# The softmax division of layer 0 moved from VectorE to GpSimd in a two-layer encoder

## The chip, the cores and the metric

The kernel runs on one core of a Trainium2 chip, in one launch. The metric is device time in microseconds: the kernel before took 577.2 us (median of 3 runs, 576.47 to 578.21).

## What is computed

A batch of one sequence of 256 tokens, 1024 wide, goes through two residual layers. Layer 0 has two attention mixers with 8 heads each (A: grouped-query, B: dilated with a relative bias), whose outputs are concatenated and projected. Layer 1 has latent attention with 16 heads. Each layer ends with a squared-ReLU MLP of width 4096. The part that the change touches is the softmax of every head:

```python
logits = jnp.einsum('bqgrd,bkgd->bgrqk', qb, k).astype(jnp.float32) * scale
p = jax.nn.softmax(logits, axis=-1).astype(v.dtype)
return jnp.einsum('bgrqk,bkgd->bqgrd', p, v)
```

In mixer B the three dilated branches are merged into one softmax over all 256 keys, with a bias on the logits.

## The kernel before

Everything is float32 accuracy. Weights come in 1 MB chunks (`raw`, L210) and are split into a high and a low part, a piece of 128x1024 at a time: ScalarE makes `whi` (L222), VectorE subtracts it from `raw` to get `wlo` (L223, two inputs, both in SBUF). Projections are three matmuls each (`mm3`, L263 to L265: high by high, high by low and low by high).

`attention` (L343) treats 16 heads of 256 queries by 256 keys in one pipeline. For a head `h`:

- `scores(h)`: TensorE writes logits, 128 queries by 256 keys twice, into a PSUM bank (tile `s`, two banks; L853 and L854, four matmuls a head in layer 0).
- `maxima(h)`: VectorE takes row maxima. For the heads of mixer A (heads 0 to 7) this is one reduction of the bank (L422) and a product with the scale (L423). For those of mixer B (heads 8 to 15) it is two fused add-and-max instructions that write the biased logits into `prob` (L870, each with a small read of its accumulator), and a negation (L873).
- `exps(h)`: ScalarE writes the exponentials into `prob`, with row sums (L427 for A, L879 for B).
- `norm(h)`: VectorE takes the reciprocals of the row sums (L365, two columns of 128) and multiplies the two 128x256 halves of `prob` by it in place (L367, twice a head).
- TensorE transposes the four 128x128 blocks of `prob` (L395, tile `o`). The first block needs the first half of `prob`, the second the second half. ScalarE copies the result to `pts` (L398).
- `values(j)`: for each pair of heads, four matmuls with the values (L384), then a high and a low part of the output (`OT`, L386 on ScalarE and L387 on VectorE).

`prob` has three buffers, so `maxima` or `exps` of head h+3 write where head h was transposed. In the loop the order of issue is: transposes of h, `scores(h+2)`, `maxima(h+2)`, `norm(h+1)`, a part of the filler, `values` of the pair before, the rest of the filler, `exps(h+2)`. The filler is work for TensorE that does not depend on the heads in hand: the value projection of mixer B (`vB`, matmuls named `mm<-..,hTs`), then the first half of the output projection (matmuls named `mm<-..,OT`).

```python
        def norm(h):
            if h < n:
                r = small(2)
                nc.vector.reciprocal(r, sums[h])
                for i in range(NT):
                    nc.vector.tensor_scalar(prob[h][:, i], prob[h][:, i], r[:, i:i + 1], None, op0=OP.mult)
```

The code is written for a scheduler: it orders the instructions of each engine at build time by what it thinks they take and by priorities (`tc.high_priority`), and adds the semaphore waits. On the chip each engine then runs its own list strictly in that order. So another engine for one step also moves the other steps. GpSimd does small work only: in layer 0 the row scales until some 43 us, then nothing until the mean square at 120 us (L331).

Of the kernel before, what the change touches and what calls it, by code (L numbers as in the profile page):

```python
# [15 lines left out]
OP = mybir.AluOpType  # L16
# [12 lines left out]
HA = 8  # L29
HB = 8  # L30
HC = 16
# [135 lines left out]
def encoder(ctx: ExitStack, tc: tile.TileContext, x, xt, wall, gcol, grow, const, onehot, relb, out):  # L167
    nc = tc.nc
# [13 lines left out]
    def s_bank():  # L182
        return psum("s", 2)

    def t_bank():
        return psum("o", 2)

    def o_bank():
        return psum("o", 2)

    def small(n, bufs=4):
        return sp.tile([P, n], F32, name=f"sm{n}", tag=f"sm{n}", bufs=bufs)
# [48 lines left out]
    def take(name, j, n, whole=True):  # L241

        i = at["take"]
        assert ORDER[i] == (name, j), (ORDER[i], name, j)
        at["take"] += 1
        while whole and at["piece"] < 4 * i + 4:
            split_piece()

        def operand(k, c=slice(None)):
            half, kk = divmod(k, n // 2)  # L250
            return tuple(z.rearrange("p (k c) -> p k c", k=n // 2)[:, kk, c] for z in parts[i, half])

        return i, operand
# [3 lines left out]
    def cols(i, n=P):  # L257
        return slice(i * n, i * n + n)
# [81 lines left out]
            nc.tensor.matmul(bank[:, which * S + t * P:which * S + t * P + P], ones, dg, start=True, stop=True)  # L340


    def attention(heads, fill, dst):  # L343
        n = len(heads)
        sb, prob, sums, pts = {}, {}, {}, {}

        def scores(h):
            if h < n:
                sb[h] = s_bank()
                heads[h]["scores"](sb[h])  # L350

        def maxima(h):
            if h < n:
                prob[h] = sp.tile([P, NT, S], F32, name="prob", tag="prob", bufs=3)
                sums[h] = small(2)
                heads[h]["max"](h, sb[h], prob[h])

        def exps(h):
            if h < n:
                heads[h]["exp"](h, sb.pop(h), prob[h], sums[h])  # L360

        def norm(h):
            if h < n:
                r = small(2)
                nc.vector.reciprocal(r, sums[h])  # L365
                for i in range(NT):
                    nc.vector.tensor_scalar(prob[h][:, i], prob[h][:, i], r[:, i:i + 1], None, op0=OP.mult)  # L367

        scores(0)
        fill(-1, 0)  # L370
        maxima(0)
        exps(0)
        scores(1)
        fill(-1, 1)
        norm(0)
        maxima(1)
        exps(1)
        def values(j):

            ob = o_bank()  # L380
            with tc.high_priority(60):
                for c in range(NT):
                    for s in range(2):
                        nc.tensor.matmul(ob[64 * s:64 * s + 64, :S], heads[2 * j + s]["v"](c),  # L384
                                         pts[2 * j + s][:, cols(c, S)], start=c == 0, stop=c == NT - 1)
            nc.scalar.copy(dst[0][:, j], ob[:, :S])  # L386
            nc.vector.tensor_tensor(dst[1][:, j], ob[:, :S], dst[0][:, j].bitcast(F32), op=OP.subtract)  # L387

        for h in range(n):
            flipped = heads[h]["flip"]  # L390
            pt = t_bank()
            for c in range(NT):
                for i in range(NT):
                    q = NT - 1 - i if flipped else i
                    turned = nc.tensor.transpose(pt[:, c * S + q * P:c * S + q * P + P], prob[h][:, i, cols(c)],  # L395
                                                 flip if flipped else ident)
            pts[h] = sp.tile([P, 512], F32, name="pts", tag="pts", bufs=3)
            nc.scalar.copy(pts[h], pt)  # L398
            with tc.high_priority(20):
                scores(h + 2)  # L400
            with tc.high_priority(100):
                maxima(h + 2)
            norm(h + 1)
            with ExitStack() as order:
                if h >= n - 2:
                    order.enter_context(tc.issue_after(turned.ins))
                fill(h, 0)
            if h % 2 == 0 and h > 0:
                values(h // 2 - 1)
            fill(h, 1)  # L410
            with tc.high_priority(20):
                exps(h + 2)
        fill(n, 0)
        values(n // 2 - 1)

    def scaled_softmax(scale, nscale):

        nb = {}

        def mx(h, sb, p):  # L420
            m, nb[h] = small(2), small(2)
            nc.vector.reduce_max(m, halves(sb), axis=AX.X)  # L422
            nc.vector.tensor_tensor(nb[h], m, nscale, op=OP.mult)  # L423

        def ex(h, sb, p, l):
            for i in range(NT):
                nc.scalar.activation(p[:, i], sb[:, cols(i, S)], AF.Exp, bias=nb[h][:, i:i + 1],  # L427
                                     scale=scale[:, i:i + 1], accum_out=l[:, i:i + 1])

        return {"max": mx, "exp": ex, "flip": False}  # L430
# [204 lines left out]
    with tc.tile_pool(name="l0", bufs=1) as lp:  # L635
# [17 lines left out]
        OT = [ap.tile([P, KT, S], F32R, name=f"OT{i}", tag=f"OT{i}") for i in range(2)]  # L653
# [13 lines left out]
        with tc.manual_schedule():  # L667
# [3 lines left out]
            for j in range(2):  # L671
                i, w = take("qA", j, 4, whole=False)
                for k in range(4):
# [5 lines left out]
                                                   op0=OP.mult, op1=OP.subtract)  # L679
# [12 lines left out]
        i, w = take("kvA", 0, 8)  # L692
# [156 lines left out]
        def scores_two(q, kd, kl, s, j, order):  # L849
            def f(sb):  # L850
                for i in range(NT):
                    o = sb[:, cols(i, S)]
                    nc.tensor.matmul(o, q[s][:, j, cols(order[i])], kd, start=True, stop=False)  # L853
                    nc.tensor.matmul(o, q[s][:, j, cols(order[i])], kl, start=False, stop=True)  # L854
            return f

        def head_a(h):
            j, s = divmod(h, 2)
            return {"scores": scores_two(qA, kdA[:, s], klA[:, s], s, j, (0, 1)),
                    "v": lambda c: vA[:, c, cols(s, 64)],  # L860
                    **scaled_softmax(fq[:, 2 * j + s], nfq[:, 2 * j + s])}

        def head_b(h):
            j, s = divmod(h, 2)
            nb = {}

            def mx(n, sb, p):
                m, nb[0] = small(2), small(2)
                for i in range(NT):
                    nc.vector.tensor_tensor_reduce(  # L870
                        out=p[:, i], in0=sb[:, cols(i, S)], in1=bias[j][:, s, i * P:i * P + S],
                        op0=OP.add, op1=OP.max, scale=1.0, scalar=-3.0e38, accum_out=m[:, i:i + 1])
                nc.vector.tensor_scalar(nb[0], m, -1.0, None, op0=OP.mult)  # L873
                if s == 1 and j < 2:
                    load_bias(j + 2)

            def ex(n, sb, p, l):
                for i in range(NT):
                    nc.scalar.activation(p[:, i], p[:, i], AF.Exp, bias=nb[0][:, i:i + 1],  # L879
                                         accum_out=l[:, i:i + 1])  # L880

            return {"scores": scores_two(qB, kdB[:, h], klB[:, h], s, j, (1, 0)), "max": mx, "exp": ex,
                    "v": lambda c: vB[:, c, cols(h, 64)], "flip": True}
# [14 lines left out]
        def fill(h, part):  # L898
            if phase[0] == 0:
                n = 1 if h < 7 else 100  # L900
            else:
                n = SHARE_AB[h - 8] if part == 0 and h < 16 else 0
            if h < 0:
                n = 1
            for _ in range(n):
                r = next(fl, None)
                if r == "second":
                    phase[0] = 1
                    return
                if r is None and n == 100:  # L910
                    return
# [7 lines left out]
            pass  # L919
        for _ in mixer_a_keys(keys[0]):  # L920
            pass
        attention([head_a(h) for h in range(HA)] + [head_b(h) for h in range(HB)], fill, OT)
        for _ in fl:
            pass

# [4 lines left out]
    with tc.tile_pool(name="l1", bufs=1) as lp:  # L930
# [8 lines left out]
        OT = [ap.tile([P, KT, S], F32R, name=f"OT{i}", tag=f"OT{i}") for i in range(2)]  # L939
# [22 lines left out]
        for j in range(2):  # L962
            i, w = take("down", j, 4)
# [114 lines left out]
        def head_c(h):  # L1078
            def scores(sb):
                for i in range(NT):  # L1080
                    nc.tensor.matmul(sb[:, cols(i, S)], qT[:, h, cols(i)], kT[:, h], start=True, stop=True)  # L1081
            return {"scores": scores, "v": lambda c: vC[:, c, cols(h, 64)], **soft}

        soft = scaled_softmax(sc, nsc)
        attention([head_c(h) for h in range(HC)], fill, OT)
        for _ in fl:
            pass

# [36 lines left out]
```

## Time and profile before

| what | value |
|---|---|
| median of 3 runs | 577.2 us |
| the profiled execution | 577.27 us |
| its span | 575.2 us |
| TensorE matmuls busy | 559.3 us (97%) |
| VectorE busy | 397.0 us (69%) |
| ScalarE busy | 329.4 us (57%) |
| GpSimd busy | 37.3 us (6%) |
| the chain that ended last, by engine | PE 86%, DVE 5%, ACT 3% |

The span runs from the first to the last instruction; the 2.1 us between it and the execution's time lie around it. A busy time is the union of an engine's instructions. Matmuls overlap and their ends are modelled, so the distance between the starts of two matmuls tells more than their lengths. In the rows below DVE is VectorE, ACT ScalarE, PE TensorE, POOL GpSimd.

### The profile page before, as it was taken

To read this page: it belongs to the slowest core of one execution; us is meant where nothing else is said; L and a number is where in the kernel's file an instruction comes from. 1 tells how busy PE (TensorE), PEld (TensorE's weight loads), DVE (VectorE), ACT (ScalarE), POOL (GpSimd) and SP (SyncE) were. 2 spreads that over 40 slices of the span, in tenths; PEclk is the share of its full clock that TensorE was granted. 3 is DMA by queue.
4 is the path that set the end of the run, shared out by engine and by line. 5 is a ranking of instruction groups with operands and counts; after the bars stand their busy time and mean duration, and the time that the engine had idled before them with its cause. 6 is when DMAs were issued, how large, how long until landed. Compare 5 with 4: busy or idle time off the path is not lost.

```text
span 575.2 us, 8125 instructions
## 1 busy us (share of the span) xinstructions
PE 559.3 (97%) x3041; PEld 462.4 (80%) x3041; DVE 397.0 (69%) x714; ACT 329.4 (57%) x610; POOL 37.3 (6%) x74
## 2 busy tenths in 40 slices
PE   7989999999999999999999999999999999999994
PEld 4889776788888888888889877678888888888884
DVE  3789997587566656656687888668566666756645
ACT  4768998465445454545556597655445454444513
POOL 3480000000000000000003100000000000000002
PEclk9989999999999999999999999999999999999998
DMA  8955463155545454554526223244545455554201
GB/s 297 404 170 200 148 228 104 73 182 184 191 175 198 173 216 156 210 188 178 195 98 221 81 98 116 74 171 158 213 154 219 162 205 169 197 206 161 74 1 73
DMA packets 16599, 96.64 MB, mean 168 GB/s; under 512 B 1922, under 2 KB 3970, under 8 KB 5808
## 3 DMA queue, kind: packets, MB, share of 16 engines
q1 hardware_dynamic: 15552, 94.64, 46.1%
q10 hardware_dynamic: 720, 0.80, 0.4%
q0 software_dynamic: 288, 0.68, 0.3%
q8 instruction: 24, 0.39, 0.3%
q14 instruction: 15, 0.12, 0.1%
HBM read 95.05 MB, written 1.06 MB: 167 GB/s over the span
## 4 chain that ended last, share of the span: by engine, by line
PE 86%; DVE 5%; ACT 3%; DMA 2%; POOL 2%; issue 1%; POOLq 0%; SPq 0%; DVEq 0%; ACTq 0%
PE s L525 19%; PE mm L263 14%; PE mm L265 14%; PE mm L264 14%; PE s L526 10%; PE o L384 3%; PE o L395 3%; PE s L1081 2%; DVE wlo L223 2%; DMA raw<-in_wall 1%; PE o L445 1%; POOL sm L318 1%; DMA xT<-in_xt 1%; PE mm L525 1%; ACT whi L222 1%
## 5 line engine op out<-in xcount | busy, mean ns | idle before, releaser
L223 DVE TENSOR_TENSOR wlo<-raw,whi 128x1024 fp32r<-128x1024 f32 (+1 forms) x182 | 208.5, 1163 | 104.6 <-ACT whi L222 104.2
L222 ACT CAST whi<-raw 128x1024 fp32r<-128x1024 f32 (+1 forms) x182 | 178.4, 1002 | 93.4 <-PE mm L265 47.8
L525 PE MATMUL s<-hTs,whi 128*128 128x512 f32 x480 | 169.7, 395 | 0.2
L526 PE MATMUL s<-hTs,wlo 128*128 128x256 f32 x480 | 134.7, 281 | 0.0
L525 PEld LDWEIGHTS s<-hTs,whi 128*128 128x128 f32 x480 | 90.0, 187 | 21.9 <-DVE hTs L453 1.1
L263 PE MATMUL mm<-whi,h2h 128*128 128x512 f32 x252 | 99.8, 396 | 0.0
L265 PE MATMUL mm<-whi,h2l 128*128 128x512 f32 x252 | 99.3, 397 | 0.0
L264 PE MATMUL mm<-wlo,h2h 128*128 128x512 f32 x252 | 99.1, 393 | 0.0
L526 PEld LDWEIGHTS s<-hTs,wlo 128*128 128x128 f32 x480 | 90.7, 189 | 1.2
L518 ACT CAST h2h<-work 128x256 fp32r<-128x256 f32 x64 | 25.7, 404 | 56.3 <-DVE work L517 56.3
L265 PEld LDWEIGHTS mm<-whi,h2l 128*128 128x128 f32 x252 | 47.3, 188 | 11.7 <-DVE h2l L519 0.3
L263 PEld LDWEIGHTS mm<-whi,h2h 128*128 128x128 f32 x252 | 47.3, 188 | 11.7 <-ACT h2h L518 0.9
L264 PEld LDWEIGHTS mm<-wlo,h2h 128*128 128x128 f32 x252 | 47.3, 188 | 10.1
L515 ACT COPY work<-s 128x256 f32<-128x256 f32 x60 | 22.0, 367 | 47.0 <-PE s L526 47.0
L516 DVE TENSOR_TENSOR work<-s,work 128x256 f32<-128x256 f32 x60 | 25.2, 420 | 17.2 <-ACT work L515 17.0
L519 DVE TENSOR_TENSOR h2l<-work,h2h 128x256 fp32r<-128x256 f32 x64 | 26.8, 422 | 14.7 <-ACT h2h L518 14.7
L517 DVE SCALAR_TENSOR_TENSOR work<-work 128x256 f32<-128x256 f32 x64 | 27.0, 424 | 2.0
L263 PE MATMUL mm<-whi,OT 128*128 128x512 f32 x64 | 26.4, 412 | 0.0
L265 PE MATMUL mm<-whi,OT 128*128 128x512 f32 x64 | 26.1, 408 | 0.0
L264 PE MATMUL mm<-wlo,OT 128*128 128x512 f32 x64 | 25.9, 405 | 0.0
L395 PE MATMUL o<-kc,prob 128*128 128x128 f32 x128 | 24.3, 281 | 1.0 <-ACT pts L398 0.7
L263 PE MATMUL mm<-whi,hTs 128*128 128x512 f32 (+1 forms) x64 | 22.1, 346 | 2.9 <-ACT hTs L677 2.9
(239 smaller groups left out, 781.0 us busy)
## 6 DMA issues: line engine op xcount, KB each, us to landing
raw<-in_wall SPq DMA_DIRECT2D x84, 1024.0 KB, 4.8
bias<-line_d SPq DMA_DIRECT2D x4, 384.0 KB, 4.2
raw<-in_wall SPq DMA_DIRECT2D x4, 256.0 KB, 5.2
raw<-in_wall SPq DMA_DIRECT2D x2, 512.0 KB, 7.7
xh<-in_x SPq DMA_DIRECT2D x1, 1024.0 KB, 12.3
xT<-in_xt SPq DMA_DIRECT2D x1, 512.0 KB, 6.7
kc<-in_const SPq DMA_DIRECT2D x1, 512.0 KB, 10.8
grw<-in_grow POOLq DMA_DIRECT2D x1, 512.0 KB, 4.1
```

Source lines behind the costliest of these rows:

```text
L222: nc.scalar.copy(hi[:, s], raw)
L223: nc.vector.tensor_tensor(lo[:, s], raw, hi[:, s].bitcast(F32), op=OP.subtract)
L263: nc.tensor.matmul(out, ah, bh, start=first, stop=False)
L264: nc.tensor.matmul(out, ah, bl, start=False, stop=False)
L265: return nc.tensor.matmul(out, al, bh, start=False, stop=last)
L395: turned = nc.tensor.transpose(pt[:, c * S + q * P:c * S + q * P + P], prob[h][:, i, cols(c)], flip if flipped else ident)
L516: nc.vector.tensor_tensor(v[:, 0], bank[:, :S], v[:, 0], op=OP.add)
L517: nc.vector.scalar_tensor_tensor(v[:, 1], v[:, 0], 0.0, v[:, 0], op0=OP.max, op1=OP.mult)
L518: nc.scalar.copy(hi, v[:, 1])
L519: nc.vector.tensor_tensor(lo, v[:, 1], hi.bitcast(F32), op=OP.subtract)
L525: nc.tensor.matmul(bank, wh, hTs[:, k].rearrange("p a t -> p (a t)"), start=k == 0, stop=False)
L526: nc.tensor.matmul(bank[:, S:], wl, hT[0][:, k], start=False, stop=k == 7)
```

## The change

`attention` gets an argument `scaler`, the engine of the two multiplications in `norm`. Layer 0 passes GpSimd, layer 1 VectorE as before. The reciprocal stays on VectorE.

```diff
-    def attention(heads, fill, dst):
+    def attention(heads, fill, dst, scaler):
...
                 r = small(2)
                 nc.vector.reciprocal(r, sums[h])
                 for i in range(NT):
-                    nc.vector.tensor_scalar(prob[h][:, i], prob[h][:, i], r[:, i:i + 1], None, op0=OP.mult)
+                    scaler.tensor_scalar(prob[h][:, i], prob[h][:, i], r[:, i:i + 1], None, op0=OP.mult)
...
-        attention([head_a(h) for h in range(HA)] + [head_b(h) for h in range(HB)], fill, OT)
+        attention([head_a(h) for h in range(HA)] + [head_b(h) for h in range(HB)], fill, OT, nc.gpsimd)
...
-        attention([head_c(h) for h in range(HC)], fill, OT)
+        attention([head_c(h) for h in range(HC)], fill, OT, nc.vector)
```

The 32 multiplications of layer 0 leave VectorE's list and stand on GpSimd's, two for each head, after its row scales and before L331. The scheduler orders the rest anew, in the attention of layer 0 above all.

On VectorE, around the reciprocals (L365) of heads 2 and 3, whose sums are `sm_679` and `sm_733`; the reductions (L422) are those of heads 4 and 5 (`sm_850`):

```order
-L223 TENSOR_TENSOR wlo<-raw,whi 128x1024
 L365 RECIPROCAL sm_738<-sm_679 128x2
-L223 TENSOR_TENSOR wlo<-raw,whi 128x1024
 L422 TENSOR_REDUCE sm_787<-s 128x2
-L367 TENSOR_SCALAR prob<-prob,sm_738 128x256
+L223 TENSOR_TENSOR wlo<-raw,whi 128x1024
 L423 TENSOR_TENSOR sm_788<-sm_787,nfq 128x2
-L367 TENSOR_SCALAR prob<-prob,sm_738 128x256
 L365 RECIPROCAL sm_791<-sm_733 128x2
 L223 TENSOR_TENSOR wlo<-raw,whi 128x1024
 L422 TENSOR_REDUCE sm_850<-s 128x2
```

The multiplications are gone, and a weight split (L223) now stands between a head's maxima (L422) and the scaling of them (L423). The reciprocal of head 3 is followed by another L223, as before.

On VectorE, around the reciprocals of heads 12 (`sm_1153`) and 13 (`sm_1197`); the L870 are those of head 14:

```order
 L365 RECIPROCAL sm_1203<-sm_1153 128x2
-L367 TENSOR_SCALAR prob<-prob,sm_1203 128x256
+L223 TENSOR_TENSOR wlo<-raw,whi 128x1024
 L870 ISA prob,sm_1223<-s,bias 128x256
 L870 ISA sm_1223 128x1
 L870 ISA prob,sm_1223<-s,bias 128x256
 L870 ISA sm_1223 128x1
-L367 TENSOR_SCALAR prob<-prob,sm_1203 128x256
 L873 TENSOR_SCALAR sm_1224<-sm_1223 128x2
-L223 TENSOR_TENSOR wlo<-raw,whi 128x1024
 L365 RECIPROCAL sm_1228<-sm_1197 128x2
```

An L223 has moved ahead, to directly behind the reciprocal of head 12.

On TensorE, behind the logits of head 5 (the last `qA_107` ahead of it). Before:

```order
L854 MATMUL s<-klA,qA_107 128x256
L263 MATMUL mm<-whi,hTs 128x512
L264 MATMUL mm<-wlo,hTs 128x512
L395 MATMUL o<-kc,prob 128x128
L384 MATMUL o<-pts,vA 64x256 x4
L395 MATMUL o<-kc,prob 128x128 x3
L265 MATMUL mm<-whi,hTs 128x512
L263 MATMUL mm<-whi,hTs 128x512
L264 MATMUL mm<-wlo,hTs 128x512
L853 MATMUL s<-kdA,qA_106 128x256
```

Now:

```order
L854 MATMUL s<-klA,qA_107 128x256
L264 MATMUL mm<-wlo,hTs 128x512
L265 MATMUL mm<-whi,hTs 128x512
L263 MATMUL mm<-whi,hTs 128x512
L264 MATMUL mm<-wlo,hTs 128x512
L395 MATMUL o<-kc,prob 128x128 x4
L265 MATMUL mm<-whi,hTs 128x512
L263 MATMUL mm<-whi,hTs 128x512
L264 MATMUL mm<-wlo,hTs 128x512
L853 MATMUL s<-kdA,qA_106 128x256
```

Before, the transposes here are those of head 2, with the values of the first pair inside, and head 3 follows among the logits of head 6. Now those of head 2 stand ahead of the logits of head 5, and the four here are those of head 3.

## Rows read from the trace of the kernel before

**Rows 1.** Page, busy time of each engine: us, share of the span, instructions.

```profile
PE 559.3 (97%) x3041; PEld 462.4 (80%) x3041; DVE 397.0 (69%) x714; ACT 329.4 (57%) x610; POOL 37.3 (6%) x74
```

**Rows 2.** Windows: length; PE, PEld, DVE, ACT, POOL busy; clock, DMA share, GB/s.

```profile
55.00:106.00 51.00, 49.86 (x299) 36.60 (x298) 42.40 (x129) 43.49 (x108) 0.00 (x0) 1.00 0.43 155
106.00:116.00 10.00, 10.00 (x48) 8.07 (x49) 7.11 (x10) 5.34 (x9) 0.00 (x0) 1.00 0.37 116
```

**Rows 3.** Timeline of PE, late starts: start, length, instruction, [idle before].

```profile
62.00 0.40 PE L263 MATMUL mm<-whi,hTs 128*128 128x512 f32 x1
62.38 0.39 PE L853 MATMUL s<-kdA,qA 128*128 128x256 f32 x1
...
95.50 0.33 PE L395 MATMUL o<-kc,prob 128*128 128x128 f32 x1
96.51 0.90 PE L395 MATMUL o<-kc,prob 128*128 128x128 f32 x3 [0.68 <-ACT pts L398]
...
98.54 0.48 PE L263 MATMUL mm<-whi,OT 128*128 128x512 f32 x1
98.95 1.08 PE L384 MATMUL o<-pts,vB 128*64 128x256 f32 x8
```

**Rows 4.** Timeline of PE, undisturbed: distances between starts.

```profile
65.38 0.28 PE L853 MATMUL s<-kdA,qA 128*128 128x256 f32 x1
65.50 0.28 PE L854 MATMUL s<-klA,qA 128*128 128x256 f32 x1
65.62 0.40 PE L264 MATMUL mm<-wlo,hTs 128*128 128x512 f32 x1
65.85 0.39 PE L265 MATMUL mm<-whi,hTs 128*128 128x512 f32 x1
...
73.94 0.27 PE L395 MATMUL o<-kc,prob 128*128 128x128 f32 x1
74.15 1.08 PE L384 MATMUL o<-pts,vA 128*64 128x256 f32 x8
75.16 0.55 PE L395 MATMUL o<-kc,prob 128*128 128x128 f32 x3
75.46 0.36 PE L853 MATMUL s<-kdA,qA 128*128 128x256 f32 x1
```

**Rows 5.** Groups of DVE, 55 to 106 us: busy us, mean ns, idle before.

```profile
L223 DVE TENSOR_TENSOR wlo<-raw,whi 128x1024 fp32r<-128x1024 f32 x12 | 14.6, 1215 | 3.1 <-ACT whi L222 3.0
L367 DVE TENSOR_SCALAR prob<-prob,sm 128x256 f32<-128x256 f32 x32 | 10.5, 348 | 0.4
L870 DVE CUSTOM_DVE_ANT_0 prob<-s,bias 128x256 f32<-128x256 f32 x16 | 6.1, 421 | 1.9 <-PE o L395 1.7
L422 DVE TENSOR_REDUCE sm<-s 128x2 f32<-128x512 f32 x8 | 5.5, 684 | 0.1
L387 DVE TENSOR_TENSOR OT<-o,OT 128x256 fp32r<-128x256 f32 x7 | 2.9, 417 | 1.7 <-ACT OT L386 1.7
L365 DVE RECIPROCAL sm<-sm 128x2 f32<-128x2 f32 x16 | 2.5, 158 | 0.1
```

**Rows 6.** Groups of POOL, the whole span: busy us, mean ns, idle before.

```profile
L601 POOL TENSOR_TENSOR y<-xh,grw 128x512 f32<-128x512 f32 x2 | 2.6, 1294 | 171.5 <-DVE xh L595 171.5
L743 POOL TENSOR_TENSOR early<-kc,early 128x32 f32<-128x32 f32 x4 | 1.4, 360 | 0.0
L659 POOL MEMSET klA<- 64x256 f32 x2 | 0.6, 308 | 0.1
L321 POOL TENSOR_SCALAR sm<-sm 128x8 f32<-128x8 f32 x2 | 0.4, 197 | 0.1
```

**Rows 7.** Timelines of POOL and of DVE, 40 to 43 us.

```profile
40.55 0.20 POOL L322 TENSOR_TENSOR fa<-sm,sm 128x8 f32<-128x8 f32 x1
...
41.28 1.07 POOL L322 TENSOR_TENSOR fa<-sm,sm 128x8 f32<-128x8 f32 x1
42.44 0.27 POOL L758 TENSOR_SCALAR fq<-fa 128x16 f32<-128x16 f32 x1
...
41.07 1.22 DVE L223 TENSOR_TENSOR wlo<-raw,whi 128x1024 fp32r<-128x1024 f32 x1
```

**Rows 8.** Timelines of DVE and of POOL: a handoff from the one to the other.

```profile
568.82 0.21 DVE L622 TENSOR_SCALAR sm<-sm,sm 128x1 f32<-128x1 f32 x1 [0.23 <-ACT junk L598]
...
569.11 0.94 POOL L623 TENSOR_TENSOR sm<-sm,mhalf 128x1 f32<-128x1 f32 x1 [1.61 <-DVE sm L622]
```

## The prediction

> **What bounds the kernel now.** I read the busy times first [rows 1]: TensorE is 97% busy, so time is won or lost only where it starts late. The windows show the stage of the change [rows 2]: in the 51 us of layer 0's attention TensorE is idle for 51.00 - 49.86 = 1.14 us, and in the ten microseconds behind it for none, all at a granted clock of 1.00. VectorE is busy for 42.4 of the 51 us and ScalarE for 43.5, so the heads run with little slack on three engines at once. Since the ends of matmuls are modelled, I then went through the starts. An undisturbed matmul with 512 columns is followed after 0.23 us, one of logits with 256 after 0.12, and a head's four transposes with a pair's values inside take 75.46 - 73.94 = 1.52 us [rows 4]. Against these steps seven starts are late by over 0.14 us. The first is at 62.38, by 0.38 - 0.23 = 0.15; the largest at 96.51, by 1.01 - 0.11 = 0.90, put down to ScalarE's `pts`; the last at 98.95, by 0.41 - 0.23 = 0.18 [rows 3]. The seven sum to 2.3 us. **That is all that this change can win**: a faster VectorE is of no use elsewhere, where the matmuls stand back to back.
>
> **What is removed.** VectorE loses 32 multiplications, 10.5 us of its busy time in the stage [rows 5]. Its reciprocal of a head (L365) and the weight splits (L223) no longer stand behind the multiplications of the head before. The old order is gone with them, and so I take its late starts out in full: **-2.3 us**. That is generous, since some were ScalarE's.
>
> **What is added.** GpSimd gets 32 multiplications of 128x256 with one input. No such row exists before. The lower end is a write without a read: 64x256 took 308 ns, so 0.31 us. The upper end is an operation with two inputs: 128x32 took 360 ns and 128x512 1294, which is 1.95 ns a column, and at 256 columns 0.80 us [rows 6]. The fixed part is about 0.20 us (128x8 took 197 ns), and with one read instead of two I take half of the 1.95 ns: 0.20 + 256 x 0.98 = **0.45 us** each, against 0.33 on VectorE (10.5 / 32). I take this value as it has the right number of inputs; the ends stay for the range. A handoff from VectorE to GpSimd took 569.11 - 569.03 = 0.08 us [rows 8]. Together GpSimd is busy for 32 x 0.45 = 14.4 us more in a stage in which it did nothing [rows 2], so its throughput is no limit: 0.9 us a head, at about 2.7 us a head. What counts is when each head's transposes find their halves ready.
>
> **The lock.** What happens where the two engines meet can be seen in one place [rows 7]. The same 128x8 operation took GpSimd 0.20 us at 40.55 and 1.07 us at 41.28, where it began inside an L223 that ran from 41.07 to 42.29; it ended at 42.35, just behind it, and the L223 itself was not longer than others (1.22 against a mean of 1.215 [rows 5]). So I count a multiplication that meets an L223 as held until the L223 ends. The Trainium skill says the same (SBUF — State Buffer, Who interferes with whom): a VectorE instruction with two SBUF inputs and a GpSimd instruction that reads SBUF exclude each other, and whoever starts second blocks. By that rule L422, L870 and L387, which read PSUM, leave GpSimd alone; the trace agrees for L223, and no run here shows the others. Without any such exclusion the sum below would be 2.3 us lower, 575.6 us.
>
> **The new waits, head by head.** The new order gives TensorE as much other work between a head's logits and its transposes as the scheduler thought it needed. For mixer A the reciprocal of head h stands behind the maxima of head h+1. From the end of the logits of h+1 that is 0.16 (the last matmul's length over its step) + L422 0.68 + L223 1.22 + L423 0.15 + L365 0.16 = 2.4 us [rows 4, 5] (the 0.15 is taken as an L365). Then come 0.08 for the handoff and 0.9 for two multiplications: 3.4 us.
> - Heads 2, 4, 5 and 6: TensorE has 3.9, 3.2, 3.6 and 3.4 us of work there (for head 6: three fillers 0.69, four transposes 0.41, five fillers 1.15, logits 0.47, three fillers 0.69). Head 4 has no L223 in its chain and needs 2.6. So nothing, or slack under 0.2, at heads 5 and 6.
> - Head 3: an L223 stands directly behind its reciprocal and gets there before GpSimd does: 3.4 + 1.22 = 4.6 us needed. TensorE has three fillers 0.69 + 1.52 + logits 0.47 + four fillers 0.92 = 3.6. Late by about **1.0 us**.
> - Head 12 likewise: from head 13's logits 0.16 + L870 twice 0.84 + L387 0.42 + 0.16 + L365 0.16 + L223 1.22 + 0.9 = 3.9 us. TensorE has four fillers 0.92, logits and two fillers 0.93, the transposes of head 11 0.41 and logits 0.47: 2.7. Late by about **1.2 us**; without the lock it would just fit. Heads 11 and 15 also have an L223 there, but over 4.5 us of other work.
> - Four heads come out with 0 to 0.2 us of slack (5, 6, 8 and 10). ScalarE, which makes `pts`, the exponentials and `whi` in turn, has no spare time in the first half, so I add 0.2 us each for its delays: **0.8 us**. The `prob` buffers close the loop: a late transpose holds L870 three heads on, and with it VectorE's list; this is inside that allowance.
>
> In the other direction GpSimd can hold an L223 for up to 0.9 us. VectorE then has 51 - 42.4 + 10.5 = 19.1 us to spare in the stage [rows 2, 5], which covers it, except where that L223 lies in a chain above. GpSimd's next own work, at 120 us, is untouched; SyncE's loads keep their order but for one bias load that passes a weight load, and wait for nothing of GpSimd.
>
> **The sum**: -2.3 + 1.0 + 1.2 + 0.8 = +0.7 us on the profiled execution's 577.27, which stands at the median of 577.2: **577.9 us**. By what a measurement of this kernel can tell, 0.3% or 1.7 us, that is no change.
>
> **Rivals.**
> - *Relief wins.* The L223 behind the reciprocals find their `whi` not yet made by ScalarE, GpSimd goes first, and its multiplication lies near 0.31 us: the terms 1.0 and 1.2 go, the 0.8 shrinks to 0.2, and 577.27 - 2.3 + 0.2 = 575.2 us. For it: L223 idled 3.0 us for ScalarE in this stage [rows 5]. Against it: seven late starts must all go, and the largest belongs to ScalarE [rows 3]. The Trainium skill leans this way (GPSIMD Engine Reference, Engine selection): one-input work on GpSimd runs at roughly line rate, which would put the multiplication near the lower end; no row before shows one. Chance 0.13.
> - *TensorE falls into step with GpSimd.* A head's logits follow the transposes of an earlier head, so a shortfall comes back at each head. The point is the multiplication's length. Each 0.1 us more costs 0.2 us at each of some six tight heads, 1.2 us together, so from about 0.55 us on the kernel is measurably slower. At 0.80 us two take 0.7 us more: head 3 late by 1.7, 12 by 1.9, 5, 6, 8 and 10 by 0.6 to 0.8 each, 9 and 13 by 0.3, together 7.0, and 577.27 - 2.3 + 7.0 = 582.0 us. For it: the two-input rows [rows 6], and that the order leaves tight heads hardly any slack. Against it: one input less. Chance 0.28.
> - *The lock works against VectorE.* GpSimd's multiplications hold the L223 in the chains of heads 2, 3, 5 and 6 by one length, 0.45 us each: 1.8 us more than forecast, 579.7 us. Against it: the old L223 was not delayed [rows 7], and L223 there waits for the next logits. Chance 0.09.
>
> **How the numbers follow.** The forecast gets 0.50; its own range is 575.9 to 578.9. The others have 0.13, 0.28 and 0.09. The range reaches from the relief's 575.2 to the step's 582.0, which leaves out a little at both sides. Faster by over 0.3% is 0.13, within it 0.50, slower 0.37.
>
> **What would show it.** In the profile of the changed kernel L367 on GpSimd should have a shortest length of about 0.45 us, and a second group above 1 us, at heads 3 and 12, beside an L223. VectorE should be busy some 10 us less, with its idle time grown by as much. TensorE's late starts should stand at L395 with GpSimd as releaser, 3 us in all, and none behind 106 us. A shortest length over 0.55 us, or late starts at nearly every head, makes the forecast wrong upward; late starts under 1 us in all, wrong downward.

## The result and the profile after

The changed kernel took 582.7 us (median of 4 runs, 582.58 to 582.96) beside 577.71 us for the kernel before in the same comparison: 1.0097 times as long, 95% interval 1.0083 to 1.0111. So it is slower by about 1%, and 0.7 us above the stated range. The profiled execution has a span of 580.6 us, 5.4 us more than before.

Busy times of the engines, from the page of the kernel after, and windows over the attention of layer 0 and what follows (columns as in [rows 2]):

```profile
PE 561.6 (97%) x3041; PEld 463.6 (80%) x3041; DVE 389.7 (67%) x682; ACT 329.1 (57%) x610; POOL 68.3 (12%) x106
```

```profile
55.00:106.00 51.00, 45.87 (x273) 32.94 (x272) 33.33 (x96) 41.56 (x105) 31.50 (x32) 1.00 0.37 133
106.00:116.00 10.00, 10.00 (x48) 7.05 (x47) 4.00 (x5) 3.79 (x7) 0.00 (x0) 1.00 0.33 117
```

VectorE is relieved as planned: 33.3 us busy in the stage instead of 42.4 [rows 2]. But TensorE is idle for 51.00 - 45.87 = 5.13 us instead of 1.14, and behind the stage for none, as before. The loss lies wholly inside the stage, at the granted clock of 1.00. GpSimd is busy for 31.5 us where 14.4 were expected. The multiplications themselves, all instructions of their line (shortest, median and longest ns; first and last start):

```profile
L367 POOL TENSOR_SCALAR prob<-prob,sm x32: 917/924/1961, 59.3 to 102.9; 128x256 f32<-128x256 f32 x32
```

**Each takes 0.92 us, twice the 0.45 that I had put in, and more than the upper end of 0.80.** Who waited for whom in the stage (us in total, times, longest):

```profile
PEld o L395 <- POOL prob L367: 9.5, 16, 1.2
ACT pts L398 <- PE o L395: 6.6, 7, 1.8
...
PE o L395 <- POOL prob L367: 5.1, 11, 0.9
DVE sm L873 <- POOL prob L367: 4.8, 6, 1.0
```

TensorE now waits at the transposes for GpSimd, 11 times (and its weight loads 16 times). I went through the starts as in the prediction: 13 are late by over 0.14 us, together 7.5 us against 2.2 us in six by the same count before. (The prediction's 2.3 us in seven takes in the start at 98.95 [rows 3]; here the starts of the values right behind a transpose, late by under 0.2 us each in every kernel, are left out on both sides.) The difference of 5.3 us is, within 0.1 us, the 5.4 us of the span. Twelve of the 13, 7.3 us, stand at L395: the 11 of the row above, and one of 0.2 us at head 9 that begins just behind the end of GpSimd's second multiplication. Head 8 shows how, on TensorE's timeline:

```profile
84.88 0.40 PE L263 MATMUL mm<-whi,OT 128*128 128x512 f32 x1
85.56 0.33 PE L395 MATMUL o<-kc,prob 128*128 128x128 f32 x1 [0.28 <-POOL prob L367]
86.46 0.55 PE L395 MATMUL o<-kc,prob 128*128 128x128 f32 x3 [0.57 <-POOL prob L367]
86.76 0.48 PE L264 MATMUL mm<-wlo,OT 128*128 128x512 f32 x1
```

The first block starts when the first half is ready, 0.68 - 0.23 = 0.45 us late; the second comes 0.90 us after it instead of 0.11, one GpSimd multiplication later, and everything behind it on TensorE waits too. At heads 2, 4 and 6 the values of a pair stand between the two blocks and cover this; at 0, 3, 8, 10 and 12 they don't, and 0.8 us or more is lost each time between the blocks alone.

### The profile page after: what moved, and what is told of

It is laid out like the page before. It is cut to its first block, busy times and chain, and to the rows that moved or that the text cites. A ratio compares the mean times of both kernels' runs of the same rounds, so it can differ in the third digit from the quotient of the medians.

```text
span 580.6 us, 8160 instructions
## 1 busy us (share of the span) xinstructions
PE 561.6 (97%) x3041; PEld 463.6 (80%) x3041; DVE 389.7 (67%) x682; ACT 329.1 (57%) x610; POOL 68.3 (12%) x106
## 4 chain that ended last, share of the span: by engine, by line
PE 87%; POOL 5%; DVE 2%; ACT 2%; issue 2%; DMA 1%; POOLq 0%; ACTq 0%; DVEq 0%
PE s L525 19%; PE mm L265 15%; PE mm L263 15%; PE mm L264 15%; PE s L526 10%; POOL prob L367 3%; PE o L395 2%; PE o L384 2%; PE s L1081 2%; PE o L445 1%; DMA g<-in_gcol 1%; POOL sm L318 1%; DVE wlo L223 1%; PE mm L525 1%; ACT prob L427 1%
## 5 line engine op out<-in xcount | busy, mean ns | idle before, releaser
L223 DVE TENSOR_TENSOR wlo<-raw,whi 128x1024 fp32r<-128x1024 f32 (+1 forms) x182 | 208.9, 1165 | 106.4 <-ACT whi L222 106.0
L367 POOL TENSOR_SCALAR prob<-prob,sm 128x256 f32<-128x256 f32 x32 | 31.5, 996 | 29.3 <-issue 16.3
L395 PE MATMUL o<-kc,prob 128*128 128x128 f32 x128 | 24.8, 285 | 5.1 <-POOL prob L367 5.1
L395 PEld LDWEIGHTS o<-kc,prob 128*128 128x128 f32 x128 | 14.9, 140 | 15.8 <-POOL prob L367 9.5
L263 PE MATMUL mm<-whi,OT 128*128 128x512 f32 x64 | 26.0, 407 | 0.0
```

The costliest lines, as they stand in the source:

```text
L223: nc.vector.tensor_tensor(lo[:, s], raw, hi[:, s].bitcast(F32), op=OP.subtract)
L263: nc.tensor.matmul(out, ah, bh, start=first, stop=False)
L367: scaler.tensor_scalar(prob[h][:, i], prob[h][:, i], r[:, i:i + 1], None, op0=OP.mult)
```

## The experiments

I had three theories: the **length** of the multiplications (TensorE falls into step, the second rival), the **lock** between L223 and GpSimd, and a **ring** that the profile after showed first. VectorE's negation L873 waited 4.8 us for GpSimd, though it touches nothing of L367. The two-column tiles for sums, maxima, negations and reciprocals share four buffers, so a reciprocal that GpSimd still reads can hold up a later head. Beside these stood the new order that the scheduler made of the other engines. Changes are shown against the changed kernel, unless told otherwise. In `quarter_cols`, `half_cols`, `constant` and `no_division` part of the division is left out, as each expectation says.

On the new order the traces themselves say something. In three pairs TensorE, VectorE and ScalarE run the same list, instruction by instruction: the changed kernel and `two_products`, `quarter_cols` and `half_cols`, `second_half` and `half_product`. In each pair only GpSimd's instruction differs. Most other comparisons, those with the kernel before above all, change the order too.

**The reciprocals in a ring of their own (own_ring).**

```diff
-                r = small(2)
+                r = sp.tile([P, 2], F32, name="rec", tag="rec", bufs=4)
```

> The reciprocals get a ring of buffers of their own, so a negation (L873) on VectorE no longer waits until GpSimd has read an old reciprocal. Theory of the ring (GpSimd and VectorE's list take turns in mixer B, one head every 2.3 us): the 4.8 us of waits of L873 for L367 go, and with them the late starts at heads 8, 10, 12 and 14 (1.2 + 0.8 + 1.4 + 0.5 = 3.9 us), so about 579 us. Theory of the length (two multiplications of 0.92 us, and TensorE waits for the second one): those late starts stay at 0.8 to 0.9 us each wherever TensorE comes early, so 581.5 to 582.7 us. Theory of the lock (GpSimd held by L223): unchanged, 582.7 us.

Measured 582.87 us, 1.0099 of the kernel before (1.0078 to 1.012): nothing gained. The waits of L873 are gone, but TensorE's late starts at L395 sum to 7.8 us, and VectorE now waits at L870:

```profile
PE o L395 <- POOL prob L367: 5.5, 11, 0.9
DVE prob L870 <- POOL prob L367: 3.9, 3, 1.8
```

At heads 8, 10, 12 and 14, where the ring theory saw all the late starts go, 3.2 of 4.0 us are left, so the ring is not what makes them late. That it cost nothing is not shown: the order is another one here, heads 0, 1 and 5 are later by 1.6 us together, and an L223 holds four multiplications instead of three.

**Fewer columns for GpSimd (quarter_cols, half_cols).**

```diff
+                w = 64 if scaler is nc.gpsimd else S
                 for i in range(NT):
-                    scaler.tensor_scalar(prob[h][:, i], prob[h][:, i], r[:, i:i + 1], None, op0=OP.mult)
+                    scaler.tensor_scalar(prob[h][:, i, :w], prob[h][:, i, :w], r[:, i:i + 1], None, op0=OP.mult)
```

`half_cols` has 128 in place of 64.

> GpSimd divides only 64 of the 256 columns of each half; the other columns stay undivided. The two lengths (256 columns take 0.92 us) give fixed part and price of a column; I expect 0.30 to 0.40 us. Theory of the length: with 0.7 us a head, as on VectorE, about 577 us. Theory of the lock: a hit still costs up to 1.0 us at three heads, 579 to 580 us. If the new order costs it and not the length: 581 us or more.

> GpSimd divides 128 of the 256 columns of each half; the other columns stay undivided. From 64 columns (0.445 us) and 256 (0.924 us) the length should be 0.445 + 64 x 2.5 ns = 0.60 us. Theory of the length (each 0.1 us beyond the forecast's 0.45 costs 1.2 us, as the prediction worked out): 577.8 + 1.5 x 1.2 = 579.6 us. If the cost comes in one step, when the two multiplications no longer fit beside a head's pace, 578 us here. Theory of the lock: as with 64 columns, 577.8 us.

Measured: with 64 columns 577.84 us, 1.0026 of the kernel before (1.0015 to 1.0036); with 128 columns 579.24 us, 1.0056 (1.004 to 1.0072). The lengths, from the instructions of the line in each, 64 columns and then 128:

```profile
L368 POOL TENSOR_SCALAR prob<-prob,sm x32: 439/446/1239, 58.7 to 98.0; 128x64 f32<-128x64 f32 x32
```

```profile
L368 POOL TENSOR_SCALAR prob<-prob,sm x32: 596/603/1398, 59.0 to 99.8; 128x128 f32<-128x128 f32 x32
```

446, 603 and 924 ns for 64, 128 and 256 columns lie on a line: 2.5 ns a column and 0.29 us fixed (0.30 to 0.40 us had been expected for 64). With 64 columns the instruction happens to have the 0.45 us of the forecast, and the kernel then stands 0.26%, 1.5 us, above the one before, where the forecast had 0.7. From there each 0.1 us of length costs about 1.1 us (0.0030 x 576 = 1.7 us for 0.157), in one and the same order. TensorE's late starts grow by as much, from 3.0 to 4.7 us.

**A product instead of a multiplication by a per-row scalar (two_products, one_product).**

```diff
-                    scaler.tensor_scalar(prob[h][:, i], prob[h][:, i], r[:, i:i + 1], None, op0=OP.mult)
+                    if scaler is nc.gpsimd:
+                        scaler.tensor_tensor(prob[h][:, i], prob[h][:, i], r[:, i:i + 1].to_broadcast([P, S]),
+                                             op=OP.mult)
```

`one_product` does both halves in one instruction: `scaler.tensor_tensor(prob[h], prob[h], r[:, :, None].to_broadcast([P, NT, S]), op=OP.mult)`.

> GpSimd divides both halves in one product of two operands (128x512, the reciprocal broadcast), in place of two multiplications by a per-row scalar. From the 128x512 product of the kernel before it should take 1.29 us, against 1.85 for the two. Theory of the length: a head is ready 0.55 us earlier, some ten late starts shrink by up to 0.5 us each, about 579 us. Theory of the ring: the turns shorten by 0.55 us in mixer B, about 580 us. Theory of the lock: a product with two inputs is held as before, at three heads, 582 us.

> Each of GpSimd's multiplications by a per-row scalar becomes a product with the broadcast reciprocal (128x256 each). The product of 128x512 took 1.04 us, so I expect 0.55 us for each. Theory of the length: whatever the kind of instruction, the time follows the length: 577.8 + 1.0 x 1.2 = 579 us. If the order that the scheduler made for GpSimd is the cause, it stays at 581 us or more.

Measured: one product 578.24 us, 1.0028 (1.0016 to 1.0039); two products 579.46 us, 1.0061 (1.0045 to 1.0076). The instructions of 128x512 and of 128x256:

```profile
L367 POOL TENSOR_TENSOR prob<-prob,sm x16: 1041/1042/1876, 59.0 to 100.3; 128x512 f32<-128x512 f32 x16
```

```profile
L368 POOL TENSOR_TENSOR prob<-prob,sm x32: 606/613/1595, 58.2 to 98.5; 128x256 f32<-128x256 f32 x32
```

The same result takes GpSimd 0.61 us for a half as a product with two inputs, against 0.92 with one input and a scalar. Two products of 0.61 us give 0.61% more time, two multiplications of 0.60 us (`half_cols`) 0.56%: **the time follows the length and not the kind**. The changed kernel and `two_products` share their order, so the fall from 0.97% to 0.61% comes from GpSimd's instruction alone; `half_cols`, with another order and kind but the same length, comes out like `two_products`. One product for both halves, 1.04 us where 1.29 was expected, does still better. A head is then complete after 1.04 us instead of 1.22, though the first block must wait for all of it; but the order differs here too, so that this is the reason is not shown.

**Is it the per-row scalar? (constant).**

```diff
-                    scaler.tensor_scalar(prob[h][:, i], prob[h][:, i], r[:, i:i + 1], None, op0=OP.mult)
+                    scaler.tensor_scalar(prob[h][:, i], prob[h][:, i], 1.0 if scaler is nc.gpsimd else r[:, i:i + 1], None, op0=OP.mult)
```

> GpSimd multiplies by the constant 1 in place of the reciprocals: the division of layer 0 is left out. If the per-row scalar makes the instruction long, it now takes 0.45 to 0.55 us, like a product, and the kernel some 578 us. If every multiplication of this kind takes that long, 0.92 us, and the kernel stays within 1 us of 582.7 (the wait for the reciprocal falls away, 0.3 us a head, which TensorE sees only where it waits).

```profile
L367 POOL TENSOR_SCALAR prob<-prob x32: 842/848/1933, 57.8 to 99.4; 128x256 f32<-128x256 f32 x32
```

0.85 us against 0.92: most of the length belongs to this kind of instruction, whatever the scalar. The one execution took 578.92 us, outside what either case expected, though the instruction is nearly as long. GpSimd no longer waits for the reciprocals and begins earlier, which the expectation had counted as little, and the order of the other engines is another one; the kernel leaves out more than the price of the scalar, and I draw no more from its time.

**The halves side by side (second_half, half_product).** VectorE divides the first half, GpSimd the second, as a multiplication or as a product.

```diff
-                    scaler.tensor_scalar(prob[h][:, i], prob[h][:, i], r[:, i:i + 1], None, op0=OP.mult)
+                    (scaler if i else nc.vector).tensor_scalar(prob[h][:, i], prob[h][:, i], r[:, i:i + 1], None, op0=OP.mult)
```

`half_product` does this too, with the product of `two_products` for GpSimd's half.

> VectorE divides the first half of a head (0.33 us), GpSimd only the second (0.92 us), side by side. Theory of the length: both halves are ready about 1.0 us behind the reciprocal instead of 1.9, the late starts fall from 7.7 us to about 2.5, so about 577.5 us. Theory of the lock: up to 1.0 us at each of three heads stays, about 580 us. If the new order of the other engines costs it, 581 us or more.

> VectorE divides the first half (0.35 us), GpSimd the second as a product (0.55 us), side by side. Theory of the length: both halves are ready 0.65 us behind the reciprocal, as early as with VectorE alone, and VectorE has 5 us less to do: 575.5 to 576.5 us, at or a little below the kernel before (576.5). If GpSimd beside VectorE slows VectorE's own multiplication (0.55 instead of 0.35 us at two heads of the run before), 576.5 to 577.5 us.

Measured: with a multiplication 576.51 us, 0.9995 (0.9984 to 1.0007), no change from the kernel before; **with a product 574.68 us, 0.9966 (0.9954 to 0.9979), faster than the kernel before and the changed one**, and below both expected ranges. The windows of half_product, layer 0's attention to 112 us and then layer 1's:

```profile
55.00:112.00 57.00, 56.99 (x333) 42.45 (x332) 43.94 (x119) 46.66 (x113) 11.50 (x16) 1.00 0.41 149
330.00:390.00 60.00, 59.73 (x334) 44.72 (x333) 45.18 (x106) 44.97 (x110) 1.77 (x3) 1.00 0.29 101
```

TensorE is idle for 0.01 us in layer 0's attention; three late starts of 0.5 us in all are left. The two runs share their order, so the 0.29% between them comes from GpSimd's instruction alone. Against the kernel before the reason is less clear. Beside VectorE the product has a median of 0.69 us and starts 0.17 us behind the reciprocal, so GpSimd's half is ready some 0.16 us later than VectorE's second one would be (an estimate, 0.86 against 2 x 0.35). So by this estimate the gain does not come from earlier halves; VectorE's list is shorter by 16 multiplications and in another order, and which of the two counts was not tried.

**What there is to win (no_division), and layer 1 (half_both).** The first is the kernel before with the loop over L367 emptied for layer 0; the second is half_product with the same split for layer 1.

```diff
-                for i in range(NT):
+                for i in range(NT if divide else 0):
```

> The kernel before without the 32 multiplications of layer 0 on any engine; the reciprocals stay, and the probabilities of layer 0 are not divided. This is the most that moving them can win. The prediction's bound says 2.3 us (the late starts of the kernel before): 573.9 us beside 576.2. If VectorE's time were worth more than TensorE's late starts show, 572 us or less; if the schedule settles into the same waits on ScalarE, 575 us.

> The split of half_product (first half on VectorE, second half as a product on GpSimd) in layer 1 too. In layer 1 a head's transposes found their halves ready in time before, so nothing is to be won there: 574.0 to 575.0 us, as half_product. If VectorE is a bound there too, 573 us; if the lock or GpSimd's 0.61 us delays heads there, 576 us or more.

Measured: without the division 575.48 us, 0.9973 (0.9964 to 0.9982), so **leaving the division out altogether brought 1.0 to 2.1 us**, in the one order that the scheduler made for it; half_product gets as much within its interval. Splitting layer 1 too gives 575.94 us, 0.9984 (0.9973 to 0.9994): still faster than before. Its interval just overlaps that of half_product, so that part of the gain is given back, against the expectation, is likely and not shown. The windows of half_both show where TensorE loses more:

```profile
55.00:112.00 57.00, 56.99 (x336) 42.62 (x335) 43.94 (x119) 47.24 (x114) 11.49 (x16) 1.00 0.43 150
330.00:390.00 60.00, 59.10 (x329) 43.58 (x328) 40.83 (x91) 44.51 (x110) 13.18 (x18) 1.00 0.30 108
```

Layer 0 is the same, and in layer 1, where the order changed too, TensorE is idle for 0.90 us instead of 0.27. The longest of these waits, 0.47 us, is one for VectorE's own half (L371, the multiplication's line there), not for GpSimd's.

## Why the prediction was wrong

**The step that failed is the price of one multiplication in "What is added".** I took 0.45 us, worked out as 0.20 us plus half the 1.95 ns a column of a two-input product, because a multiplication has one input instead of two. It measured 0.92 us, 0.29 fixed and 2.5 ns a column. The upper end of 0.80 was not an end, since it came from another kind of instruction: the rows of before had products and memsets at hundreds of columns, but multiplications by a scalar at 2 to 16 columns only [rows 6]. "One input less" pointed the wrong way: the product of this size, whose second input is one value a row repeated, takes 0.61 us. The Trainium skill (GPSIMD Engine Reference, Engine selection), which has one-input work at roughly line rate and two-input work at about half of VectorE's, leaned the same way; the runs disagree for this pair, 0.92 us with one input against 0.61 with two.

The other steps, point by point:

- *What bounds the kernel, and the most that can be won.* Right. The bound of 2.3 us was to be a little generous, and without any division 1.0 to 2.1 us are gained; TensorE's late starts fall from 2.2 to 0.6 us there.
- *The mechanism and its slope.* Right. The second rival, TensorE in step with GpSimd, is what happened: from about 0.55 us on the kernel was to be measurably slower, by 1.2 us for each further 0.1. It is so at 0.60 us (1.0056), and the slope there is 1.1. Its price of 582.0 us was worked out for 0.80 us. From 0.61 to 0.92 us, in the changed kernel's own order, the slope is lower, (1.0097 - 1.0061) x 577 = 2.1 us for 0.31, so 0.7 for each 0.1. It had a chance of 0.28, and slower by over 0.3% had 0.37: too little for a price without a row of its kind.
- *The forecast at its own price.* At 0.45 us it had 0.7 us for the change; the kernel with 64 columns shows 1.5 (0.9 to 2.1). Its late starts are 3.0 us, which is what the sum had put in (1.0 + 1.2 + 0.8), but not where: they stand at heads 0, 10, 11 and 14. So this agreement is luck. About 1.2 of the 3.0 us are two multiplications that VectorE held, one of head 10 by an L223 (1.24 us long) and one of head 0 by another subtraction with two SBUF inputs (0.90 us). Head 0 was not in my list of tight heads, which began at head 2.
- *Which heads.* Of the two that were to meet an L223, head 3 was late by 1.0 us as written, head 12 by 0.65 + 0.79 = 1.4 (1.2 written). At head 3 the number is luck in part: the L223 waited for ScalarE's `whi` and came behind the first multiplication (70.36 against 70.12), so only the second was held, for 0.5 us, and the length made up the rest. Of the four with little slack, 5, 8 and 10 were late (0.4, 1.2 and 0.8) and 6 was not. Heads 0, 1 and 14 came as a surprise, with 1.4, 0.4 and 0.5: nearly a third of the 7.3 us stands at heads that the sum put at nothing.
- *The handoff.* It was taken as 0.08 us and measured 0.16 to 0.19 us at all 15 heads where GpSimd stood idle, as at head 13 (VectorE, then GpSimd): 97.94 - 97.78 = 0.16 us.

```profile
97.62 0.16 DVE L365 RECIPROCAL sm<-sm 128x2 f32<-128x2 f32 x1
```

```profile
97.94 0.93 POOL L367 TENSOR_SCALAR prob<-prob,sm 128x256 f32<-128x256 f32 x1 [0.44 <-DVE sm L365]
```

- *A slip in the sums.* The two lock terms, 1.0 and 1.2, come to 2.2 us; the section on the lock has 2.3.
- *The lock.* It is there, but is the smaller part. Three multiplications of 32 are held: their lengths are 1.44, 1.96 and 1.72 us. At head 11 this cost nothing. At heads 3 and 12 it lengthened the wait by up to 0.5 and 0.8 us, 1.3 of the 7.3 us. This is read from the rows below; a kernel without the collisions was not tried. The other half of the reading held as well: 11 multiplications that began inside an L422, L870 or L387 took 917 to 926 ns like the rest. The third rival, the lock against VectorE, did not show: an L223 took 1.31 us at most, instead of 1.22.

The held multiplications of heads 3, 11 and 12 on GpSimd's timeline, and the L223 that the last two met on VectorE's:

```profile
71.02 1.44 POOL L367 TENSOR_SCALAR prob<-prob,sm 128x256 f32<-128x256 f32 x1
...
91.55 1.96 POOL L367 TENSOR_SCALAR prob<-prob,sm 128x256 f32<-128x256 f32 x1 [0.44 <-DVE sm L365]
...
94.89 1.72 POOL L367 TENSOR_SCALAR prob<-prob,sm 128x256 f32<-128x256 f32 x1 [0.47 <-DVE sm L365]
```

```profile
91.50 1.23 DVE L223 TENSOR_TENSOR wlo<-raw,whi 128x1024 fp32r<-128x1024 f32 x1
...
94.61 1.21 DVE L223 TENSOR_TENSOR wlo<-raw,whi 128x1024 fp32r<-128x1024 f32 x1
```

At head 11 the multiplication ends at 93.51, 0.78 us behind its L223 (92.73); at head 12 at 96.61, 0.79 us behind 95.82. A held multiplication starts nearly afresh when the L223 ends, as the prediction counted it.

## What to carry to other kernels

Where a scheduler has fitted an engine's work just in time, moving a step to an idle engine helps only if the step is no longer there than its old wait: the engine's throughput had room to spare, and the latency cost 1%. Take the price of a moved step from a row of the same kind of instruction, and where there is none, let the range and the chances say so. And before giving a whole step away, try a split: VectorE and GpSimd side by side, each with one half, gave 0.34%, about as much as leaving the step out gave.

## What the runs showed of the hardware

- On GpSimd a product of 128x256 with a broadcast operand (0.61 us) is shorter than a multiplication of 128x256 by a per-row scalar (0.92 us) or by a constant (0.85 us). The 128x512 product with the broadcast took 1.04 us, against 1.29 for one with two full operands [rows 6].
- The exclusion between the two engines works both ways, but not for the same time. A multiplication that begins inside an L223 waits for its end. An L223 that begins inside a multiplication is hardly lengthened: 1.31 us instead of 1.22, where the multiplication had some 0.7 us still to go (VectorE, then GpSimd, at head 3):

```profile
70.36 1.31 DVE L223 TENSOR_TENSOR wlo<-raw,whi 128x1024 fp32r<-128x1024 f32 x1 [0.43 <-ACT whi L222]
```

```profile
70.12 0.92 POOL L367 TENSOR_SCALAR prob<-prob,sm 128x256 f32<-128x256 f32 x1 [0.96 <-DVE sm L365]
```

  A product on GpSimd holds an L223 for longer. In one_product one took 1.62 us that began 0.5 us into a product of 1.04 (VectorE, then GpSimd):

```profile
75.17 1.62 DVE L223 TENSOR_TENSOR wlo<-raw,whi 128x1024 fp32r<-128x1024 f32 x1 [0.67 <-ACT whi L222]
```

```profile
74.67 1.04 POOL L367 TENSOR_TENSOR prob<-prob,sm 128x512 f32<-128x512 f32 x1 [1.49 <-DVE sm L365]
```

  It ends 1.08 us behind the product (76.79 and 75.71), wherever it began: the same 1.08 us stands in all eight cases of `one_product`, `two_products`, `half_product` and `half_both` in which the product had more than 0.3 us to go. Behind a multiplication by a scalar an L223 with some 0.7 us or more to go ended 0.62 us behind it (twice here, once in `constant`), and with less than 0.5 us to go it was not lengthened. So it is as if the multiplication let go 0.46 us earlier before its recorded end than the product does.

  The Trainium skill (SBUF — State Buffer, Who interferes with whom) has whoever issues first keep the pair for the whole instruction, and the other block fully. That holds here for GpSimd behind an L223 and for an L223 behind a product, but not up to the recorded end of a multiplication by a scalar.
- In second_half a VectorE multiplication, which has one input and took 0.35 us otherwise, took 0.55 us when it began inside one of GpSimd's, VectorE first:

```profile
66.38 0.55 DVE L367 TENSOR_SCALAR prob<-prob,sm 128x256 f32<-128x256 f32 x1
```

```profile
65.86 0.93 POOL L367 TENSOR_SCALAR prob<-prob,sm 128x256 f32<-128x256 f32 x1 [1.32 <-PE o L395]
```

  In half_product two that began inside a product took 0.40 and 0.56 us, and both ended 0.15 us behind its end. This VectorE instruction costs 0.53 ns a column (280 ns for 128 columns at L339, 348 for 256), about half of L223's 1.2 us for 1024. What the two engines share there was not looked into.
